# A two-layer hybrid decoder on one core: row and table loads on SyncE's queue, a merged last FFN group, compress in two column halves, and a new issue order

## The chip, the core and the metric

The kernel runs on one core of a Trainium2 chip. The core has five engines that run in parallel, each with its own in-order instruction stream: TensorE (PE, the matmul array; its weight load is listed apart as PEld), VectorE (DVE), ScalarE (ACT), GpSimd (POOL) and SyncE (SP), which here only starts transfers. Sixteen DMA engines move data between HBM and the on-chip memory SBUF; matmuls write to PSUM. The metric is the time of one execution on the device, in microseconds (us); less is better.

## The reference

Two consecutive decoder layers over 256 tokens of 1024 features, in fp32:

```python
for l in range(DEPTH):                                   # 2
    x = LN(a*x + 0.5 * swiglu(x, ffn1_w1, ffn1_w3, ffn1_w2))   # 1024 -> 2816 -> 1024
    z = x @ w_in + b_in                                  # split into 20 parts
    y_a = gmlp(u, v)                                     # causal spatial gating in chunks of 128
    y_b = short_conv(cb, cc, ch)                         # gated convolution, 3 taps
    y_c = mla(q_lat, kv_lat, k_rope)                     # latent attention, 8 heads
    y_d = nsa(nq, nkc, nvc, nks, nvs, nkw, nvw, ngate)   # compressed + selected + window attention
    x = LN(a*x + (sum_i sigmoid(g_i) * y_i) @ w_o)
    x = LN(a*x + cross_attention(x, mem))                # 4 heads, 256 memory rows
    x = LN(a*x + 0.5 * swiglu(x, ffn2_w1, ffn2_w3, ffn2_w2))
```

Inside `nsa`, 15 overlapping blocks of 32 keys and of 32 values are each compressed to one vector for each of two groups: `k_cmp = einsum('bnlgd,lde->bnge', k_blocks + pe_k, wcmp_k)`, and likewise for v. The rows of the result are 2 x 15 = 30, with 64 columns.

## The kernel before

The 256 tokens are two tiles (t = 0, 1) of 128 partitions. All fp32 matmuls of the dense layers are three matmuls of a split form: an operand is a high part (h) and a low part (l), and `mm3` (lines 245 to 250) issues high by high (L248), high by low (L249) and low by high (L250).

**Weights.** `unit` brings a piece of a weight matrix in tiles of 128 x 1024: SP issues the transfer into `raw` (L233, 4 buffers, 0.5 MB), ACT casts it to the high part `wh` (L236), DVE subtracts to the low part `wl` (L237); wh and wl are rings of 8 tiles. `ffn` runs over six column groups of w1 and w3, five of 512 columns and the last of 256; in each group it computes both products for both token tiles, ACT takes silu (L383), DVE multiplies (L385), PE transposes the result (L298), and `wide` multiplies it with w2 into four PSUM tiles (2 token tiles x 2 halves of 512 columns). Weight matrices after that: `z` (the input projections, part by part, each with a bias row), the mixers' projections, `w_o`, cross-attention, the second FFN.

**Small loads.** `row` broadcasts a vector (a bias, the scales gg, gb, qg, and lng and lnb of a layer norm) to 128 partitions; `small` loads a table (ws and bs of the gMLP, cw of the convolution, pek, pev and the compress weights wc). They are issued on POOL, except lng and lnb, which `ln_params` issues on SP. The four pieces of the memory (`memr`, L859) are issued on POOL too. POOL computes besides these only the reciprocal roots of the layer norms (L319) and some gate sums (L814).

**Compress** (lines 556 to 607). For k, and then for v: PE transposes with the 128 x 64 halves of the identity's columns (L569), DVE adds the position table (L579), 16 matmuls with K = 128, 30 stationary columns (kcp) and 64 streamed columns (wc) accumulate into the first 30 partitions of an `att` PSUM tile (L582), and ACT copies it out. k then gets its rotary embedding on DVE, a transpose (L593) and a mask; v is spread to 120 rows by a matmul with a 0/1 matrix `sel` (L600).

**PSUM**: `acc` has 3 buffers, `oacc` 1, `tr` 2, `att` 2, each 128 x 512.

**Order.** Every engine's instruction order is fixed by the table `ISSUE`, which `issue_order` (L965) turns into dependences: for each engine a permutation of its instructions as written. A scheduler chooses nothing here. SP's table gives the order of all transfers on SP's queue; an SP instruction that waits (for a free raw buffer, or a free row buffer) holds those behind it. Around the places that the change moves, in the order of time in layer 0: FFN 1 to about 190 us, its layer norm LN1, the input projections from about 200 us, compress near 280 us, the attention of nsa up to 352 us, the paired transposes of MLA's queries and keys (`mq`, `mk`, in `mla_up`) near 375 us, w_o from 500 us, cross-attention near 570 us, FFN 2 from 587 us. Layer 1 repeats this some 764 us later.

## Time and profile before

| | |
|---|---|
| time, median of 3 runs | 1549.39 us (1548.55 to 1550.39) |
| the profiled execution | 1547.46 us, of which span 1545.6 us |
| granted PE clock, mean | 0.994 of full speed |
| busy: PE / DVE / ACT / POOL | 1501.9 / 1003.0 / 721.0 / 92.2 us |
| SP's DMA queue (q1) | 262.62 MB, 51.3% of the 16 engines' time |
| POOL's DMA queue (q0) | 14.79 MB, 3.8% |

The span is the time from the first to the last instruction on the core, and busy shares are of it. A matmul's duration in a row is longer than the distance to the next one's start, since matmuls overlap in the array; the pace is read from the starts. In a row of the timeline, "x4" means four instructions in one row, and a bracket gives the engine's idle time before it and what ended it.

### The profile page before, as it was taken

The page shows a single profiled execution, that of the slowest core. Times are in us where ns is not written, and L with a number is a line of the kernel's source. Part 1 is how long each engine was busy: PE and PEld are TensorE (multiplying, and loading weights), DVE is VectorE, ACT ScalarE, POOL GpSimd, SP SyncE. Part 2 cuts the span into 40 slices and gives each one's busy share as a digit, 9 for nine tenths or more (in the row PEclk, how much of TensorE's full clock was granted, in tenths as well). Part 3 has the DMA queues.
Part 4 walks back from the last instruction along what each step waited for, and adds up shares of the span by engine and source line. Part 5 has one row for each costly group of instructions (what it writes and reads, how often), then busy time and mean ns, then how long its engine had stood idle before and what let it go on. Part 6 is the DMA issues. An engine that isn't in the chain of part 4 may idle for free.

```text
span 1545.6 us, 20575 instructions
## 1 busy us (share of the span) xinstructions
PE 1501.9 (97%) x7798; PEld 1251.0 (81%) x7798; DVE 1003.0 (65%) x1426; ACT 721.0 (47%) x1060; POOL 92.2 (6%) x116
## 2 busy tenths in 40 slices
PE   7999999998999999999999999999999999999997
PEld 6888878877787888888878888888777888888886
DVE  5556468887865857555566555688878577665644
ACT  5435335554644454444345443355556444544531
POOL 0000011100121000000000000120001300000000
PEclk9999999999999999999999999999999999999999
DMA  8567566434466455556475565764245655356551
GB/s 310 174 205 219 183 210 201 151 100 130 157 206 209 157 184 178 172 173 213 164 231 189 175 214 172 244 192 153 86 145 168 212 191 189 124 191 205 187 188 61
DMA packets 78482, 278.78 MB, mean 180 GB/s; under 512 B 9328, under 2 KB 10032, under 8 KB 78384
## 3 DMA queue, kind: packets, MB, share of 16 engines
q1 hardware_dynamic: 73440, 262.62, 51.3%
q0 software_dynamic: 4800, 14.79, 3.8%
q8 instruction: 61, 1.00, 0.2%
q14 instruction: 37, 0.30, 0.1%
q10 hardware_dynamic: 144, 0.07, 0.0%
HBM read 276.39 MB, written 1.05 MB: 180 GB/s over the span
## 4 chain that ended last, share of the span: by engine, by line
PE 88%; DVE 4%; ACT 3%; DMA 3%; issue 1%; POOLq 0%; ACTq 0%; SPq 0%; DVEq 0%
PE acc L248 23%; PE acc L250 22%; PE acc L249 22%; PE oacc L250 4%; PE oacc L249 4%; PE oacc L248 4%; PE tr L298 3%; DMA raw<-in_wflat_dram 3%; ACT wh L236 2%; PE att L469 1%; DVE wl L237 1%; PE acc L298 1%; PE oacc L482 1%; DVE e L453 1%; PE att L582 0%
## 5 line engine op out<-in xcount | busy, mean ns | idle before, releaser
L237 DVE TENSOR_TENSOR wl<-raw,wh 128x1024 fp32r<-128x1024 f32 (+2 forms) x486 | 581.4, 1208 | 263.4 <-ACT wh L236 254.1
L236 ACT CAST wh<-raw 128x1024 fp32r<-128x1024 f32 (+2 forms) x486 | 501.6, 1041 | 515.8 <-PE acc L250 193.6
L248 PE MATMUL acc<-wh,xh 128*128 128x512 f32 (+3 forms) x1200 | 464.0, 388 | 16.1 <-ACT wh L236 6.9
L249 PE MATMUL acc<-wl,xh 128*128 128x512 f32 (+3 forms) x1200 | 458.6, 383 | 0.0
L250 PE MATMUL acc<-wh,xl 128*128 128x512 f32 (+3 forms) x1200 | 457.0, 382 | 0.1
L248 PEld LDWEIGHTS acc<-wh,xh 128*128 128x128 f32 x1200 | 227.2, 189 | 59.3 <-ACT wh L236 8.6
L250 PEld LDWEIGHTS acc<-wh,xl 128*128 128x128 f32 x1200 | 227.0, 189 | 42.1 <-DVE xl L284 1.6
L249 PEld LDWEIGHTS acc<-wl,xh 128*128 128x128 f32 x1200 | 227.6, 190 | 38.7 <-issue 0.7
L249 PE MATMUL acc<-wl,hh 128*128 128x512 f32 x264 | 103.1, 391 | 0.0
L248 PE MATMUL acc<-wh,hh 128*128 128x512 f32 x264 | 102.8, 389 | 0.0
L250 PE MATMUL acc<-wh,hl 128*128 128x512 f32 x264 | 102.7, 389 | 0.0
L385 DVE SCALAR_TENSOR_TENSOR h<-acc,sil 128x512 f32<-128x512 f32 (+1 forms) x24 | 15.5, 647 | 99.5 <-PE acc L250 99.5
L319 POOL TENSOR_TENSOR rstd<-var,cst 128x1 f32<-128x1 f32 x28 | 28.1, 1004 | 835.1 <-DVE var L318 835.0
L249 PE MATMUL oacc<-wl,xh 128*128 128x512 f32 (+1 forms) x208 | 77.5, 373 | 0.0
L248 PE MATMUL oacc<-wh,xh 128*128 128x512 f32 (+1 forms) x208 | 77.5, 373 | 0.0
L250 PE MATMUL oacc<-wh,xl 128*128 128x512 f32 (+1 forms) x208 | 77.5, 373 | 0.0
L248 PEld LDWEIGHTS acc<-wh,hh 128*128 128x128 f32 x264 | 49.6, 188 | 10.3
L250 PEld LDWEIGHTS acc<-wh,hl 128*128 128x128 f32 x264 | 49.6, 188 | 10.1
L249 PEld LDWEIGHTS acc<-wl,hh 128*128 128x128 f32 x264 | 49.6, 188 | 10.0
L444 ACT ACTIVATE e<-att,nm 128x256 f32<-128x256 f32 (+1 forms) x112 | 46.9, 430 | 9.6 <-DVE nm L440 7.9
L383 ACT ACTIVATE sil<-acc 128x512 f32<-128x512 f32 (+1 forms) x48 | 27.0, 563 | 38.5 <-PE acc L250 38.5
L476 ACT COPY pT<-tr 128x512 f32<-128x512 f32 x36 | 21.1, 586 | 51.1 <-PE tr L298 51.0
(262 smaller groups left out, 1791.7 us busy)
## 6 DMA issues: line engine op xcount, KB each, us to landing
raw<-in_wflat_dram SPq DMA_DIRECT2D x466, 512.0 KB, 5.0
bias<-in_rows_dram POOLq DMA_DIRECT2D x30, 256.0 KB, 4.7
lng<-in_rows_dram SPq DMA_DIRECT2D x8, 512.0 KB, 6.1
lnb<-in_rows_dram SPq DMA_DIRECT2D x8, 512.0 KB, 6.8
raw<-in_wflat_dram SPq DMA_DIRECT2D x8, 416.0 KB, 8.2
wc<-in_small_dram POOLq DMA_DIRECT2D x8, 256.0 KB, 6.0
memr<-in_mem_dram POOLq DMA_DIRECT2D x8, 256.0 KB, 5.4
raw<-in_wflat_dram SPq DMA_DIRECT2D x4, 420.0 KB, 3.9
```

The source lines that it names most:

```text
L236: nc.scalar.copy(hi[:, :m], raw[:, :m])
L237: nc.vector.tensor_sub(lo[:, :m], raw[:, :m], hi[:, :m])
L248: mm(out, ah, bh, start=start, stop=False, skip_group_check=True)
L249: mm(out, ah, bl, start=False, stop=False, skip_group_check=True)
L250: mm(out, al, bh, start=False, stop=stop, skip_group_check=True)
L298: self.nc.tensor.transpose(t[:rows, i * part:(i + 1) * part], s, self.ident[:part, :part])
L319: nc.gpsimd.tensor_tensor(y, v, self.c("mhalf"), op=ALU.pow)
L383: nc.scalar.activation(sil, pa[:, :w], AF.Silu)
L385: nc.vector.scalar_tensor_tensor(h, pb[:, :w], 0.5, sil, op0=ALU.mult, op1=ALU.mult)
L444: nc.scalar.activation(e[:, h * keys:(h + 1) * keys], ps[:, h * keys:(h + 1) * keys], AF.Exp, bias=nm[:, h:h + 1], scale=scale, accum_out= ...
L453: nc.vector.tensor_mul(ev, ev, r[:, :, None].to_broadcast([P, heads, keys]))
L476: nc.scalar.copy(pTs[-1], pt)
```

## The change

Five edits:

- `row`, `small` and the `memr` loads are issued on SP (`nc.sync`) and not on POOL. SP's rows in the order go from 510 to 578, POOL's from 121 to 53.
- The last column group of each FFN takes 256 columns of w1 and 256 of w3 as one unit of 512, into one `acc` tile; silu reads its left half, the product its right half.
- `compress` prepares k and v first, then interleaves their 32 matmuls: k into partitions 0 to 29, v into 64 to 93 of one `att` tile. `sel` moves to partitions 64 to 93.
- `wide` takes (acc, oacc) for t = 0 and (acc, acc) for t = 1 (before: the other way round), and pending transposes are flushed after each of its blocks rather than all before it.
- `ISSUE` is new for all five engines.

```diff
-    def row(self, name, l, o, w, dst, queue=None):
+    def row(self, name, l, o, w, dst):
         base = l * ROW_TOTAL + ROW_OFF[name] + o
-        (queue or self.nc.gpsimd).dma_start(dst, self.a["rows"][0:1, base:base + w].to_broadcast([P, w]))
+        self.nc.sync.dma_start(dst, self.a["rows"][0:1, base:base + w].to_broadcast([P, w]))
...
-        self.nc.gpsimd.dma_start(dst, self.a["small"][:, o:o + w])
+        self.nc.sync.dma_start(dst, self.a["small"][:, o:o + w])
...
-        widths = [512] * 5 + [256]
...
+        for gi in range(6):
+            c0 = gi * 512
+            w = min(512, FF - c0)
+            if w == 512:
+                u1 = self.cols(w1, l, c0, w, KD)
+                u3 = self.cols(w3, l, c0, w, KD)
+            else:
+                u13 = self.cols((w1, w3), l, c0, 2 * w, KD)
             for t in range(NT):
-                pa, pb = self.acc(), self.acc() if t == 0 else self.oacc()
                 self.stream = "af"[t]
-                self.group(pa[:, :w], self.xT[t], u1, 0, w)
-                self.group(pb[:, :w], self.xT[t], u3, 0, w)
+                if w == 512:
+                    pa, pb = self.acc(), self.acc() if t == 0 else self.oacc()
+                    self.group(pa, self.xT[t], u1, 0, w)
+                    self.group(pb, self.xT[t], u3, 0, w)
+                else:
+                    both = self.acc()
+                    self.group(both, self.xT[t], u13, 0, 2 * w)
+                    pa, pb = both[:, :w], both[:, w:]
...
-        self.flush(True)
...
-            po = self.att()
-            for k in range(16):
-                nc.tensor.matmul(po[:30, :64], kcp[:, k * 30:(k + 1) * 30], w[k // 8][:, k % 8 * 64:(k % 8 + 1) * 64],
-                                 start=k == 0, stop=k == 15, skip_group_check=True)
...
+            parts.append((kcp, S[nmw]))
+        po = self.att()
+        for k in range(16):
+            for i, (kcp, w) in enumerate(parts):
+                nc.tensor.matmul(po[64 * i:64 * i + 30, :64], kcp[:, k * 30:(k + 1) * 30],
+                                 w[k // 8][:, k % 8 * 64:(k % 8 + 1) * 64], start=k == 0, stop=k == 15,
+                                 skip_group_check=True)
...
-        out = {t: [self.acc(), self.acc() if t == 0 else self.oacc()] for t in range(NT)}
+        out = {t: [self.acc(), self.oacc() if t == 0 else self.acc()] for t in range(NT)}
...
+                self.flush(True)
...
-                nc.gpsimd.dma_start(mt[t, q], self.a["mem"][t * P:(t + 1) * P, q * 512:(q + 1) * 512])
+                nc.sync.dma_start(mt[t, q], self.a["mem"][t * P:(t + 1) * P, q * 512:(q + 1) * 512])
...
-        "4 0 5-6 1 7 2-3 48-49 8-47 50-78 159-160 79-158 161-172 175-180 173 181 174 182-196 231-232 197-230 "
...
+        "4 0 5-6 1-2 7-47 3 48 50 49 51-58 72 59-61 77 62-71 73-76 78-79 90-92 105 84 87 80 93 81 96-99 101-104 "
```

At the start, SP's order had the constants (cst), lng and lnb right behind the first few weight tiles; now the three stand behind the tiles of the first FFN's w1 and w3. At the end of layer 0's FFN 1, SP issues the first tiles of the input projections (128x1024; those of 128x832 belong to the next part). Its order there was before:

```order
L233 DMA raw_1612<-in_wflat_dram 128x1024
L233 DMA raw_1618<-in_wflat_dram 128x1024
L233 DMA raw_1624<-in_wflat_dram 128x1024
L213 DMA lng_4448<-in_rows_dram 128x1024
L213 DMA lnb_4449<-in_rows_dram 128x1024
L233 DMA raw_1630<-in_wflat_dram 128x1024
L233 DMA raw_1771<-in_wflat_dram 128x832
L233 DMA raw_1777<-in_wflat_dram 128x832
```

and the loads of POOL at that point (two qg, four wc, two bias) were in a queue of their own. Now it is:

```order
L233 DMA raw_1562<-in_wflat_dram 128x1024
L233 DMA raw_1568<-in_wflat_dram 128x1024
L213 DMA gg_1709<-in_rows_dram 128x512
L213 DMA gb_1710<-in_rows_dram 128x512
L218 DMA ws_1711<-in_small_dram 128x512
L213 DMA bias_2073<-in_rows_dram 128x512
L218 DMA pek_1697<-in_small_dram 128x16
L218 DMA pev_1703<-in_small_dram 128x16
L233 DMA raw_1574<-in_wflat_dram 128x1024
L218 DMA bs_1712<-in_small_dram 128x4
L233 DMA raw_1580<-in_wflat_dram 128x1024
```

LN2's lng and lnb are gone from here (they come after the mixers' weights), and gg, gb, ws, one bias, pek, pev and bs have come in, most of them ahead of the tile next to last of the eight (raw_1574; raw_1624 before); qg and wc follow some 20 tiles later.

On PE, compress before had k's 16 products (two rows of 8, by the two wc tiles) ahead of a transpose, with v's behind it (not in this piece):

```order
L250 MATMUL acc_3150<-wh_3110,xl_1569 128x512
L582 MATMUL att_2056<-wc_1749,kcp_2053 30x64 x8
L582 MATMUL att_2056<-wc_1750,kcp_2053 30x64 x8
L697 MATMUL acc_3160<-zv_2203,ws_1761 128x128 x4
L248 MATMUL acc_3150<-wh_3110,xh_1568 128x512
L249 MATMUL acc_3150<-wl_3111,xh_1568 128x512
L250 MATMUL acc_3150<-wh_3110,xl_1569 128x512
L593 MATMUL tr_2083<-ident,cmp_2073 128x30
```

Now k's and v's alternate, here the last of 32, after 32 matmuls of 512 columns since the transposes, and followed by the window attention's scores:

```order
L589 MATMUL att_2021<-wc_1700,kcp_2003 30x64
L589 MATMUL att_2021<-wc_1706,kcp_2018 30x64
L589 MATMUL att_2021<-wc_1700,kcp_2003 30x64
L589 MATMUL att_2021<-wc_1706,kcp_2018 30x64
L250 MATMUL acc_3160<-wh_3156,xl_1488 128x512
L250 MATMUL acc_3196<-wh_3138,xl_1519 128x512
L248 MATMUL acc_3196<-wh_3138,xh_1518 128x512
L474 MATMUL att_2154<-kT_1901,qT_1896 128x128
```

What moved: the products of v came up beside those of k, and the transpose of the compressed keys (L600 now) stands behind eight scores and five matmuls.

On PE, at the end of the nsa attention of layer 0, the products with the values (oacc), the scores with the compressed keys (kcT), the transposes of the exponentials e and the next input projection stood in a row:

```order
L482 MATMUL oacc_2365<-pT_2515,zzd_1927 64x128
L482 MATMUL oacc_2365<-pT_2536,zzd_1927 64x128
L527 MATMUL att_2606<-kcT_2085,qT_1973 128x30 x4
L298 MATMUL tr_2570<-ident,e_2561 128x128 x4
L248 MATMUL acc_3576<-wh_3554,xh_1537 128x512
L249 MATMUL acc_3576<-wl_3555,xh_1537 128x512
L250 MATMUL acc_3576<-wh_3554,xl_1538 128x512
```

Now projection matmuls stand between them:

```order
L487 MATMUL oacc_2313<-pT_2484,zzd_1877 64x128
L248 MATMUL acc_3524<-wh_3502,xh_1487 128x512
L249 MATMUL acc_3524<-wl_3503,xh_1487 128x512
L250 MATMUL acc_3524<-wh_3502,xl_1488 128x512
L248 MATMUL acc_3524<-wh_3502,xh_1487 128x512
L532 MATMUL att_2554<-kcT_2067,qT_1923 128x30 x4
L249 MATMUL acc_3524<-wl_3503,xh_1487 128x512
L250 MATMUL acc_3524<-wh_3502,xl_1488 128x512
...
L250 MATMUL acc_3524<-wh_3508,xl_1488 128x512
L248 MATMUL acc_3524<-wh_3514,xh_1487 128x512
L298 MATMUL tr_2518<-ident,e_2509 128x128 x4
```

Four stand between the products and the scores, and nine between the scores and the transposes; ahead of this piece, two transposes of e, eight scores and eight products follow each other with no projection between. In MLA, the second of the pairs of transposes (tr mq, tr mk) has five projection matmuls between its halves now, and none before; the first pair is as it was. In cross-attention, two output-projection matmuls now stand ahead of the second product with the memory's values (L931 before). The four memr loads stand in SP's order between w_o's fifth and sixth weight tiles.

## Rows read from the trace of the kernel before

**Rows 1.** The page: busy time of each engine; the chain that ended last

```profile
PE 1501.9 (97%) x7798; PEld 1251.0 (81%) x7798; DVE 1003.0 (65%) x1426; ACT 721.0 (47%) x1060; POOL 92.2 (6%) x116
...
PE 88%; DVE 4%; ACT 3%; DMA 3%; issue 1%; POOLq 0%; ACTq 0%; SPq 0%; DVEq 0%
```

**Rows 2.** Timeline of PE in FFN 1: start us, us, instruction, shape, count

```profile
113.52 0.39 PE L249 MATMUL acc<-wl,xh 128*128 128x512 f32 x1
...
114.20 0.39 PE L249 MATMUL acc<-wl,xh 128*128 128x512 f32 x1
...
126.24 0.28 PE L250 MATMUL acc<-wh,xl 128*128 128x256 f32 x1
...
126.96 0.28 PE L250 MATMUL acc<-wh,xl 128*128 128x256 f32 x1
```

**Rows 3.** Timeline of PE: compress, a column-tiled transpose, an untiled product (cross-attention)

```profile
278.86 1.97 PE L582 MATMUL att<-wc,kcp 128*30 128x64 f32 x32
...
282.71 1.09 PE L569 MATMUL tr<-ident,zzb 128*64 128x128 f32 x16
...
569.25 2.05 PE L931 MATMUL acc<-xpT,XV 128*128 128x128 f32 x16 [0.29 <-ACT xpT L927]
```

**Rows 4.** Timelines of SP's queue and of PE at the start

```profile
5.54 0.33 SPq L948 DMA_DIRECT2D cst<-in_consts_dram  x1
...
18.17 0.72 PE L248 MATMUL acc<-wh,xh 128*128 128x512 f32 x2 [1.62 <-ACT wh L236]
```

**Rows 5.** Timelines of POOL's and SP's queues as LN1 ends

```profile
202.94 2.12 POOL L218 DMA_DIRECT2D wc<-in_small_dram  x4
...
203.94 0.33 SPq L213 DMA_DIRECT2D lng<-in_rows_dram  x1
```

**Rows 6.** The chain through that stretch: start us, us, what

```profile
206.49 8.67 DMA raw<-in_wflat_dram
```

**Rows 7.** The page: landing time of weight loads; the cast of a tile

```profile
raw<-in_wflat_dram SPq DMA_DIRECT2D x466, 512.0 KB, 5.0
...
L236 ACT CAST wh<-raw 128x1024 fp32r<-128x1024 f32 (+2 forms) x486 | 501.6, 1041 | 515.8 <-PE acc L250 193.6
```

**Rows 8.** Timeline of PE after LN1 in both layers; in brackets the idle before

```profile
213.21 0.39 PE L248 MATMUL acc<-wh,xh 128*128 128x512 f32 x1
...
216.33 0.80 PE L248 MATMUL acc<-wh,xh 128*128 128x512 f32 x1 [2.74 <-ACT wh L236]
...
219.37 0.39 PE L248 MATMUL acc<-wh,xh 128*128 128x512 f32 x1
...
979.96 0.50 PE L248 MATMUL acc<-wh,xh 128*128 128x512 f32 x1 [2.41 <-ACT wh L236]
```

**Rows 9.** Timeline of PE: end of the sliding-window and compressed attention; an MLA pair

```profile
350.61 0.66 PE L298 MATMUL tr<-ident,e 128*128 128x128 f32 x4 [0.72 <-DVE e L453]
...
352.31 0.79 PE L248 MATMUL acc<-wh,xh 128*128 128x512 f32 x1 [1.04 <-DVE y L739]
...
353.74 0.63 PE L248 MATMUL acc<-wh,xh 128*128 128x512 f32 x1
...
379.17 0.64 PE L298 MATMUL tr<-ident,mk 128*96 128x128 f32 x4 [0.94 <-ACT mk L658]
...
380.86 0.44 PE L248 MATMUL att<-wh,lh 128*128 128x384 f32 x1 [0.28 <-ACT mq L647]
```

**Rows 10.** Timeline of PE in cross-attention and at the start of w_o

```profile
572.60 0.60 PE L931 MATMUL acc<-xpT,XV 128*128 128x128 f32 x3 [0.42 <-ACT xpT L927]
...
501.82 0.50 PE L248 MATMUL acc<-wh,xh 128*128 128x512 f32 x1 [1.54 <-ACT xh L286]
```

**Rows 11.** Table by stretch: us, busy us (instructions) by engine, clock, DMA share, GB/s

```profile
216.33:219.20 2.87, 2.87 (x7) 2.31 (x8) 2.14 (x2) 1.67 (x2) 0.00 (x0) 0.50 0.40 101
...
494.00:500.20 6.20, 6.20 (x32) 5.06 (x30) 5.96 (x9) 3.16 (x3) 0.00 (x0) 1.00 0.58 187
```

**Rows 12.** Waits of SP's queue, 196 to 218 us: total us, times, longest

```profile
SPq L213 <- DVE x L358: 5.8, 1, 5.8
```

More of the change, by code (lines that the diff above doesn't have):

```diff
@@ L98, in _constants @@
     put("cmpvalid", valid)
-    sel = np.zeros((30, 4, 2, NCMP))
+    sel = np.zeros((94, 4, 2, NCMP))
     for g in range(2):
         for n in range(NCMP):
-            sel[g * NCMP + n, :, g, n] = 1.0
+            sel[64 + g * NCMP + n, :, g, n] = 1.0
     put("sel", sel)
@@ L335, in ln_params @@
         b = self.p.tile([P, D], F32, name=self.nm("lnb"), tag="lnb", bufs=1)
-        self.row(f"ln{which}_g", l, 0, D, g, nc.sync)
-        self.row(f"ln{which}_b", l, 0, D, b, nc.sync)
+        self.row(f"ln{which}_g", l, 0, D, g)
+        self.row(f"ln{which}_b", l, 0, D, b)
         return g, b
@@ L557, in compress @@
         nc = self.nc
-        outs = []
+        parts = []
         for i, (nmw, nmp) in enumerate((("wck", "pek"), ("wcv", "pev"))):
-            w, pe = S[nmw], S[nmp]
+            pe = S[nmp]
             kc = self.s("kc2")
@@ L579, in compress @@
                 nc.vector.tensor_add(kpv[:, :, g, :], src, pe[:, :, None].to_broadcast([P, 16, NCMP]))
-            po = self.att()
-            for k in range(16):
-                nc.tensor.matmul(po[:30, :64], kcp[:, k * 30:(k + 1) * 30], w[k // 8][:, k % 8 * 64:(k % 8 + 1) * 64],
-                                 start=k == 0, stop=k == 15, skip_group_check=True)
-            c = self.s("cmp", P)[:30]
-            if i == 0:
-                kr = self.s("kraw", 64)[:30]
-                nc.scalar.copy(kr, po[:30, :64])
-                cv = c.rearrange("p (u d) -> p u d", u=2)
-                x = kr[:, None, :]
-                self.rope(cv[:, 0:1, :], x, self.c("rcc", 30), self.c("rcs", 30), 1, 32, rows=30)
-                nc.vector.tensor_copy(cv[:, 1, :], cv[:, 0, :])
-                pt = self.tr()
-                nc.tensor.transpose(pt[:, :30], c, self.ident[:30, :30])
-                kcT = self.s("kcT", 30)
-                nc.vector.tensor_mul(kcT, pt[:, :30], self.c("bd"))
-                outs.append(kcT)
-            else:
-                nc.scalar.copy(c[:, :64], po[:30, :64])
-                pr = self.tr()
-                nc.tensor.matmul(pr[:120, :64], self.c("sel", 30), c[:, :64], start=True, stop=True,
-                                 skip_group_check=True)
-                vr = self.s("vrep")[:120]
-                nc.vector.tensor_mul(vr.rearrange("p (h d) -> p h d", h=8),
-                                     pr[:120, None, :64].to_broadcast([120, 8, 64]),
-                                     self.c("blk", 120)[:, :, None].to_broadcast([120, 8, 64]))
-                outs.append(vr)
@@ L607, in compress @@
-        return outs
+            parts.append((kcp, S[nmw]))
[4 more added lines that the diff above has]
+                                 w[k // 8][:, k % 8 * 64:(k % 8 + 1) * 64], start=k == 0, stop=k == 15,
+                                 skip_group_check=True)
+        c = self.s("cmp", P)
+        kr = self.s("kraw", 64)[:30]
+        nc.scalar.copy(kr, po[:30, :64])
@@ new lines, in compress @@
+        nc.scalar.copy(c[64:94, :64], po[64:94, :64])
+        cv = c[:30].rearrange("p (u d) -> p u d", u=2)
+        self.rope(cv[:, 0:1, :], kr[:, None, :], self.c("rcc", 30), self.c("rcs", 30), 1, 32, rows=30)
+        nc.vector.tensor_copy(cv[:, 1, :], cv[:, 0, :])
+        pt = self.tr()
+        nc.tensor.transpose(pt[:, :30], c[:30], self.ident[:30, :30])
+        kcT = self.s("kcT", 30)
+        nc.vector.tensor_mul(kcT, pt[:, :30], self.c("bd"))
+        pr = self.tr()
+        nc.tensor.matmul(pr[:120, :64], self.c("sel", 94)[64:], c[64:94, :64], start=True, stop=True,
+                         skip_group_check=True)
@@ L609, in mla_latents @@
+        vr = self.s("vrep")[:120]
+        nc.vector.tensor_mul(vr.rearrange("p (h d) -> p h d", h=8),
+                             pr[:120, None, :64].to_broadcast([120, 8, 64]),
+                             self.c("blk", 120)[:, :, None].to_broadcast([120, 8, 64]))
+        return kcT, vr
     def mla_latents(self, S):
@@ L1110, in _layout, with cut @@
     W["nsa_wout"] = W["nsa_wout"][:, WOUT_ROWS, :]
+    def cut(n, l, k0, nk, c0, w):
+        if isinstance(n, tuple):
+            return np.concatenate([cut(m, l, k0, nk, c0, w // len(n)) for m in n], 1)
+        return W[n][l, k0 * P:(k0 + nk) * P, c0:c0 + w]
     flat = np.concatenate([
-        W[n][l, k0 * P:(k0 + nk) * P, c0:c0 + w].reshape(nk, P, w).transpose(1, 0, 2).reshape(-1)
-        for n, l, k0, nk, c0, w in plan])
+        cut(n, l, k0, nk, c0, w).reshape(nk, P, w).transpose(1, 0, 2).reshape(-1) for n, l, k0, nk, c0, w in plan])
     rows, small = [], []
```

10 lines of the change are left out of this document (2 added, 8 removed), and 227 rows, old and new, of the table ISSUE.

## The prediction

> **What bounds the kernel now.** I read the busy row and the chain first: TensorE (PE) works 97% of the span, and the chain that ended last is 88% PE [rows 1]. So an edit pays only if it shortens PE's own work or one of its waits; DVE, ACT and the DMA rings matter where PE waits for them. The idle time in front of PE is about 44 us (span less busy), and the timelines of PE show where it stands: a few places of 0.4 to 2.7 us that come back in both layers. The terms below are those places and the two edits to PE's work.
>
> **FFN tail, 256 to 512 columns.** Four FFNs, two token tiles, w1 and w3, eight k, three matmuls each: 384 matmuls of 256 columns go, 192 of 512 columns come. In one stretch the 256-column ones start 0.72 us apart over six, 0.120 each; the 512-column ones 0.68 apart over three, 0.227 each [rows 2]. 384 x 0.120 = 46.1 and 192 x 0.227 = 43.6: **2.5 us saved**, all on PE's path. Weight bytes stay the same. The silu and the product now wait for one group instead of two; their cover is the first blocks of w2, which need earlier h tiles, so I cost that at nothing; uncovered it would be a wait like the 0.72 to 1.04 us of [rows 9] per FFN.
>
> **Compress in two halves.** Before, k and v each run 16 matmuls, which the trace counts as 32 (two fp32 passes), in 1.97 us; two layers, so four such stretches [rows 3]. After, k writes partitions 0 to 29 and v 64 to 93, alternating. What speaks for an overlap is line 569, which alternates column halves already: 16 in 1.09 us, while the untiled line 931, with the same 128 streamed columns, takes 2.05 us for 16 [rows 3]. If the compress halves overlap as well, 4 x 1.97 becomes 2 x 1.97, less a little for the first pair: **3.6 us saved**. Bounds: at best 3.9; at worst each matmul costs what one of line 569 costs, 1.09 / 16 = 68 ns, and 128 of them take 8.7 us instead of 7.9, a loss of 0.8. I take 3.6, since 569 streams twice as many columns. The Trainium skill, "TensorEngine Tiling (Array Packing)", Instruction Overhead, speaks against it: every matmul carries some 60 cycles, and a tiling factor should not be taken from a dimension that is already small, as 64 columns and 30 weights are; by that rule the term is about zero. No run here shows so short a stream in halves. The merged compress also waits until both inputs are ready; the order has 32 matmuls of 512 columns between its transposes and its products and 13 matmuls between the products and the next transpose, so I add nothing (uncovered: one wait for e or y as below, about 1 us per layer).
>
> **The start.** The constants and, behind them, LN1's lng and lnb, 0.5 MB each, are issued ahead of a weight tile, and PE then waits 1.62 us for that tile's cast [rows 4]. In the new order all three stand behind the first FFN's w1|w3 tiles, so the tile lands 1.5 MB earlier: **1.6 us saved**. What is late next is the tile after it, which moves up alike.
>
> **After LN1, where the projections begin.** This is the largest place. Around 203 us POOL issues qg, four wc and two bias loads, and SP issues lng and lnb of LN2 [rows 5]; the weight tile issued behind them at 206.49 needs 8.67 us to land [rows 6], where the median is 5.0 [rows 7]. PE idles 2.74 us for its cast, and after that idle time it runs at a granted clock of 0.50 (1.2 instead of 2.4 GHz) [rows 11]: the seven matmuls from 216.33 to 219.37 take 3.04 us instead of 7 x 0.227 = 1.59 [rows 8]. Together 2.74 + 1.45 = 4.2. Layer 1 has the same with 2.41 idle [rows 8]: 3.9, if the low clock costs as much there. In the new SP order lng and lnb stand after the mixers' weights, qg and wc some 20 tiles later; gg, gb, ws and one bias (1 MB) stand ahead of the tile before it, but what they wait for is done earlier on PE than the release of that one, so they go out while the rings have time. With 5.0 to land from 206.49 and 1.04 for the cast [rows 7] the tile is ready at 212.5; PE needs it at 213.4. **8.0 us saved**, with 0.9 us to spare; if half of the delay stays, half of the gain is lost. The zc bias now comes later and could hold DVE's evacuation; PE has some 4 us of other groups there, so nothing is added.
>
> **End of the sliding-window and compressed attention.** Before, scores, transposes of e and the next projection stand back to back: PE idles 0.72 us for e and 1.04 us for y, and three matmuls at the low clock cost 1.43 instead of 0.68 [rows 9]. The new order puts four matmuls behind the attention products and nine or more 512-column ones between the compressed scores and the transposes of e (2 us of cover against 1.8 of idle): 0.72 + 1.04 + 0.75 = 2.5, twice: **5.0 us saved** (layer 1 taken as layer 0). But the stretch ahead of it (two transposes of e, eight scores, eight products) now has no filler: there I add two waits like the 0.72 in each layer, **2.9 us lost**; bounds 0 and 6.
>
> **MLA pairs.** tr mq and tr mk stood back to back, with 0.94 us of idle for mk and 0.28 for mq in each of two pairs [rows 9]. The first pair stays as it was; in the second five matmuls (1.1 us) stand between: 1.2, twice: **2.4 us saved**. **Cross-attention:** two output-projection matmuls now stand ahead of the second product, which waits 0.42 us [rows 10]; twice: **0.8 us saved**.
>
> **w_o.** Here the move can cost. The four memr loads (1.05 MB) went out on POOL's queue before the w_o tiles; now they stand in SP's queue among them, and PE already waits 1.54 us there [rows 10]. In the 6.2 us before that wait the rings are 0.58 busy at 187 GB/s [rows 11]: 0.42 x 6.2 us at 322 GB/s (187 / 0.58) is room for 0.84 MB; 0.21 MB is left over, 0.65 us. Bounds: nothing, or all of it, 1.05 MB at 322 GB/s = 3.3 us. I take 1.0 per layer: **2.0 us lost**.
>
> The out-tile swap in wide() and the flush in its blocks change which PSUM buffer comes free first; PE's order shows the same matmuls around the layer norms, so zero, with 1 us either way.
>
> **Sum:** 2.5 + 3.6 + 1.6 + 8.0 + 5.0 + 2.4 + 0.8 - 2.9 - 2.0 = 19.0 us. The profiled execution took 1547.46 and would take 1528.5; the median of the runs is 1.9 above it, so 1530.
>
> **Rivals.** *A, the halves do not overlap* (the change does not do what it says): +3.6, 1533.7. *B, the burst only moves.* A load is as heavy on SP's queue as on POOL's; if the 1 MB that now stands ahead of the tile is still in flight at 206, PE waits as before: +8.0, 1538. The Trainium skill, "DMA: Bandwidth & Descriptors", Issuing engines are not separate DMA queues, says that all issuers share the same 16 engines, so that only the order and not the queue can help; the row of 8.67 us agrees, and by that rule alone the change of queue gains nothing. *C, the rearranged stalls come back* (next to another product): 5.0 + 2.4 + 0.8 = 8.2, 1538. *D, slower: a row load blocks the weights.* SP issues in order; 68 more loads stand in its queue, and a load that waits for its buffer holds every weight tile behind it. The queue's own waits show it: a row load (L213) held it 5.8 us for a DVE result of the layer norm [rows 12], and the tile behind came late. Each such hold that empties the ring costs about 4.2 (idle and clock); five undo the gain, six give 1530 + 25 = 1555. Against it: in the built program nearly every row load waits for something that PE has passed before it reaches what the next weight tile waits for; the exception is lnb ahead of the last FFN, 35 matmuls later.
>
> **How the numbers follow.** 0.2% (3 us) is about what a measurement of this kernel can tell from no change. Forecast 0.50 (own range 1524 to 1536: no new waits and no loss at w_o, 4.9 less; both at their upper bounds, 3.1 and 4.6 more, one of them, and 1 of the swap); A 0.14; B 0.10; C 0.12, all faster; two or three of A to C at once, up to 1530 + 20 = 1550, 0.05 (same); D 0.09 (slower). Faster 0.86, same 0.05, slower 0.09. The range reaches from 1520 (other waits that I counted nothing for go too) to 1544 (two of the rivals at once).
>
> **What would show it.** In the profile after: 192 fewer matmuls and no 256-column form with x; compress in about 2 us per layer with starts some 28 ns apart (A: 56); no idle before PE near 18; after LN1 a tile that lands in 5 us, no PE row with an idle over 1 us there and a full granted clock (B: the same 2 to 3 us); no row of 0.72 and 1.04 before the compressed transposes, 0.5 to 0.7 before the products ahead; w_o's idle at 2 to 3 us instead of 1.54. D would show as waits of SP's queue at L213 followed by PE idle for wh. The prediction is wrong if idle of PE after stays above 35 us, or if it falls under 15.

## The result and the profile after

The changed kernel takes 1529.1 us (median of 4 runs, 1527.79 to 1532.97) against 1549.89 before: ratio 0.9871, interval 0.9851 to 0.9891. The forecast was 1530. The profiled execution took 1528.15, of which the span is 1526.4; the sum in the prediction gave 1528.5.

The page after, as in [rows 1]: busy time (share) and count of each engine, and the chain that ended last; then the group of the 512-column matmuls with the idle time in front of them and what ended most of it.

```profile
PE 1489.9 (98%) x7606; PEld 1234.3 (81%) x7606; DVE 1002.8 (66%) x1426; ACT 719.9 (47%) x1060; POOL 50.6 (3%) x48
...
PE 88%; DMA 4%; DVE 3%; ACT 3%; issue 1%; SPq 0%; POOLq 0%; POOL 0%; ACTq 0%; DVEq 0%
L248 PE MATMUL acc<-wh,xh 128*128 128x512 f32 (+2 forms) x1168 | 461.3, 396 | 8.5 <-ACT xh L286 4.2
```

192 matmuls fewer, as said. PE is busy 12.0 us less and idle 7.2 us less (span less busy: 43.7 before, 36.5 after). Half of the idle in front of the 512-column products is now for `xh`, the cast of the transposed gated sum at the start of w_o.

Where the time went by stage. A stage ends where PE starts the first matmul on the newly normalised x, a row that both timelines have (before 199.56, 540.24, 587.04, 774.81, 963.51, 1302.65, 1349.53; after 197.40, 530.38, 576.75, 764.01, 953.47, 1285.00, 1331.88); the last stage ends with the span. The column "forecast" puts the prediction's terms into their stages.

| stage | before, us | after, us | change | forecast |
|---|---|---|---|---|
| start and FFN 1, layer 0 | 199.56 | 197.40 | -2.2 | -2.2 |
| projections, mixers, w_o, layer 0 | 340.68 | 332.98 | -7.7 | -7.2 |
| cross-attention, layer 0 | 46.80 | 46.37 | -0.4 | -0.4 |
| FFN 2, layer 0 | 187.77 | 187.26 | -0.5 | -0.6 |
| FFN 1, layer 1 | 188.70 | 189.46 | +0.8 | -0.6 |
| projections, mixers, w_o, layer 1 | 339.14 | 331.53 | -7.6 | -7.0 |
| cross-attention, layer 1 | 46.88 | 46.88 | 0.0 | -0.4 |
| FFN 2, layer 1, to the end | 196.07 | 194.52 | -1.6 | -0.6 |
| sum | 1545.6 | 1526.4 | -19.2 | -19.0 |

The stages agree with the forecast to within 1.4 us each; inside the two long ones some terms are wrong, and cancel. Of the 1.6 us of the last stage, 1.0 lies behind PE's last matmul (9.8 us from its start to the end of the span before, 8.8 after, and about the same in every run of the changed kernel below); its cause is open. The rows, in the order of the prediction. First the timeline of PE after at compress and at the start (start us, us, instruction, shape, count, idle before it in brackets), the places of [rows 3] and [rows 4].

```profile
281.00 1.98 PE L589 MATMUL att<-wc,kcp 128*30 128x64 f32 x64
...
15.45 0.73 PE L248 MATMUL acc<-wh,xh 128*128 128x512 f32 x2 [0.28 <-ACT wh L236]
```

64 matmul records (the 32 products of k and v) in the time that 32 took: two column halves with 30 stationary columns and 64 streamed ones overlap fully. At the start 0.28 us of idle is left of 1.62.

The stretch behind LN1 in both layers, in the table by stretch (us, then busy us with instructions for PE, PEld, DVE, ACT, POOL, then granted clock, DMA share, GB/s), to be read against [rows 8] and [rows 11].

```profile
197.40:216.00 18.60, 18.58 (x84) 15.07 (x85) 16.45 (x23) 7.01 (x9) 0.99 (x1) 1.00 0.53 169
953.47:972.00 18.53, 18.51 (x84) 15.02 (x85) 15.88 (x22) 6.96 (x9) 0.92 (x1) 1.00 0.53 167
```

PE is busy throughout, at the full granted clock (2.4 GHz): the idles of 2.74 and 2.41 us and the seven slow matmuls behind are gone in both layers.

The end of the sliding-window attention in the timeline of PE, layer 0 (337 to 343 us) and layer 1, and the clock of the stretch behind the first two; the counterpart of [rows 9].

```profile
337.20 0.63 PE L298 MATMUL tr<-ident,e 128*128 128x128 f32 x4 [1.79 <-DVE e L458]
338.81 1.12 PE L298 MATMUL acc<-ident,zcb 128*128 128x128 f32 x4 [0.98 <-DVE y L742]
343.19 1.09 PE L487 MATMUL oacc<-pT,zzd 128*64 128x128 f32 x14 [0.31 <-ACT pT L481]
...
1093.67 1.16 PE L474 MATMUL att<-kT,qT 64*128 64x128 f32 x14 [1.74 <-ACT e L449]
...
338.80:341.90 3.10, 3.09 (x21) 2.54 (x21) 2.02 (x4) 1.14 (x5) 0.00 (x0) 0.51 0.34 52
```

The waits of 0.72 and 1.04 us ahead of and behind the compressed transposes are gone. In layer 0 the waits ahead of them, 1.79 and 0.98, are larger than those removed; in layer 1 one wait of 1.74, for ACT's e, stands for the two.

MLA in the timeline of PE, layer 0 and then layer 1; DVE's row behind the wait for T; the chain's row ahead of that (start us, us, what); and SP's queue ahead of this load.

```profile
365.75 0.61 PE L298 MATMUL tr<-ident,mq 128*96 128x128 f32 x4 [0.69 <-DVE mq L432]
367.31 0.64 PE L298 MATMUL tr<-ident,mk 128*96 128x128 f32 x4 [0.94 <-ACT mk L661]
371.62 0.50 PE L248 MATMUL acc<-wh,yah 128*128 128x512 f32 x1 [0.80 <-DVE T L802]
...
1119.89 0.64 PE L298 MATMUL tr<-ident,mk 128*96 128x128 f32 x4 [0.94 <-ACT mk L661]
1124.34 0.64 PE L298 MATMUL tr<-ident,mk 128*96 128x128 f32 x4 [0.94 <-ACT mk L661]
...
370.87 0.69 DVE L802 TENSOR_TENSOR T<-acc,bias 128x512 f32<-128x512 f32 x1 [0.94 <-DMA bias<-in_rows_dram]
...
364.62 6.23 DMA bias<-in_rows_dram
...
349.85 14.71 SPq L233 DMA_DIRECT2D raw<-in_wflat_dram  x6
```

In MLA's attention, PE before waited four times for DVE's e, twice in each layer (timeline of PE before); the changed kernel has no such wait of 0.2 us or more there.

```profile
410.94 0.63 PE L298 MATMUL tr<-ident,e 128*128 128x128 f32 x4 [0.51 <-DVE e L453]
415.95 0.63 PE L298 MATMUL tr<-ident,e 128*128 128x128 f32 x4 [0.50 <-DVE e L453]
...
1174.80 0.63 PE L298 MATMUL tr<-ident,e 128*128 128x128 f32 x4 [0.52 <-DVE e L453]
1179.57 0.63 PE L298 MATMUL tr<-ident,e 128*128 128x128 f32 x4 [0.24 <-DVE e L453]
```

The start of w_o in both layers (layer 1 before, then both after), and two waits in layer 1's FFN 1 that were not there before (timeline of PE), with DVE's rows at the first of them.

```profile
1264.64 0.50 PE L248 MATMUL acc<-wh,xh 128*128 128x512 f32 x1 [0.95 <-ACT xh L286]
...
492.11 0.50 PE L248 MATMUL acc<-wh,xh 128*128 128x512 f32 x1 [1.92 <-ACT xh L286]
1245.92 0.50 PE L248 MATMUL acc<-wh,xh 128*128 128x512 f32 x1 [2.32 <-ACT xh L286]
...
781.70 0.66 PE L298 MATMUL acc<-ident,h 128*128 128x128 f32 x4 [0.69 <-DVE h L391]
791.56 0.66 PE L298 MATMUL tr<-ident,h 128*128 128x128 f32 x4 [0.77 <-DVE h L391]
...
779.82 1.23 DVE L237 TENSOR_TENSOR wl<-raw,wh 128x1024 fp32r<-128x1024 f32 x1 [2.69 <-ACT wh L236]
780.96 0.68 DVE L391 SCALAR_TENSOR_TENSOR h<-acc,sil 128x512 f32<-128x512 f32 x1
```

### The profile page after: what moved, and what is told of

Its sections match the earlier page's. It is cut to its first block, busy times and chain, and to the rows that moved or that the text cites. A ratio compares the mean times of both kernels' runs of the same rounds, so it can differ in the third digit from the quotient of the medians.

```text
span 1526.4 us, 20113 instructions
## 1 busy us (share of the span) xinstructions
PE 1489.9 (98%) x7606; PEld 1234.3 (81%) x7606; DVE 1002.8 (66%) x1426; ACT 719.9 (47%) x1060; POOL 50.6 (3%) x48
## 4 chain that ended last, share of the span: by engine, by line
PE 88%; DMA 4%; DVE 3%; ACT 3%; issue 1%; SPq 0%; POOLq 0%; POOL 0%; ACTq 0%; DVEq 0%
PE acc L248 22%; PE acc L250 22%; PE acc L249 22%; PE oacc L248 4%; PE oacc L249 4%; PE oacc L250 4%; PE tr L298 3%; DMA raw<-in_wflat_dram 3%; DVE wl L237 2%; ACT wh L236 2%; PE att L474 2%; PE oacc L487 1%; PE acc L298 1%; PE acc L935 1%; PE att L919 0%
## 5 line engine op out<-in xcount | busy, mean ns | idle before, releaser
L248 PE MATMUL acc<-wh,xh 128*128 128x512 f32 (+2 forms) x1168 | 461.3, 396 | 8.5 <-ACT xh L286 4.2
L250 PE MATMUL acc<-wh,xl 128*128 128x512 f32 (+2 forms) x1168 | 454.9, 390 | 0.1
L249 PE MATMUL acc<-wl,xh 128*128 128x512 f32 (+2 forms) x1168 | 454.5, 390 | 0.0
L248 PEld LDWEIGHTS acc<-wh,xh 128*128 128x128 f32 x1168 | 220.0, 188 | 52.3 <-ACT xh L283 6.0
L250 PEld LDWEIGHTS acc<-wh,xl 128*128 128x128 f32 x1168 | 219.8, 188 | 44.3 <-DVE xl L284 1.6
L249 PEld LDWEIGHTS acc<-wl,xh 128*128 128x128 f32 x1168 | 220.2, 189 | 39.9 <-issue 0.2
L249 PE MATMUL oacc<-wl,xh 128*128 128x512 f32 x176 | 68.7, 390 | 0.0
L248 PE MATMUL oacc<-wh,xh 128*128 128x512 f32 x176 | 68.7, 390 | 0.0
L250 PE MATMUL oacc<-wh,xl 128*128 128x512 f32 x176 | 68.5, 389 | 0.0
L319 POOL TENSOR_TENSOR rstd<-var,cst 128x1 f32<-128x1 f32 x28 | 23.6, 846 | 1112.2 <-DVE var L318 1111.9
```

The source lines that it names most:

```text
L248: mm(out, ah, bh, start=start, stop=False, skip_group_check=True)
L249: mm(out, ah, bl, start=False, stop=False, skip_group_check=True)
L250: mm(out, al, bh, start=False, stop=stop, skip_group_check=True)
L319: nc.gpsimd.tensor_tensor(y, v, self.c("mhalf"), op=ALU.pow)
```

## The experiments

The time of one kernel moves from run to run by more than most terms are large: the two profiled executions of the changed kernel below are 4.5 us apart. So small terms are read from the row at their place, and medians where a whole kernel is compared. Where an edit of the issue order goes with a piece of code, the pieces below show the main lines alone ("..." marks what is left out).

**The changed kernel again,** beside three of the kernels below.

> The changed kernel once more, beside the three below. If the medians on record stand, 1529 us (1527 to 1533) and 19 to 20 us under the kernel before. The stalls that moved with the change should be at the same places: PE idle 1.8 and 1.0 us near 337 and 339 for e and y, 1.7 us near 1094 for e, 1.9 and 2.3 us at the start of w_o (492 and 1246). What may differ from run to run is the granted clock in the few microseconds behind such an idle: up to 3 us in all.

Measured: 1529.75 us (1525.93 to 1532.76, 5 runs), ratio 0.9884 (0.9865 to 0.9903); the kernel before, measured beside it, 1547.33. The stalls that were named are at the same places within 0.25 us (1.78 and 0.98; 1.74; 2.14 and 2.13 at w_o); the first wait for h in layer 1 is 1.14 instead of 0.69. The profiled execution is 4.5 us longer than the first one. Set against the first matmul by matmul, 2.7 us of it lie where the granted clock differs: 1.5 behind w_o's wait in layer 0 and 1.2 behind the wait of 1.74 us in layer 1. Another 1.2 lie at the start, where the matmuls stand 0.43 us apart until 10.6 us in the first profile and until 13.0 us in this one. An example of the clock is the stretch behind the wait of 1.74 us (PE goes on at 1093.67 and at 1097.44) in the table by stretch, first the earlier profile, then this one.

```profile
1093.60:1097.00 3.40, 3.02 (x32) 2.49 (x34) 3.30 (x10) 1.75 (x6) 0.00 (x0) 1.00 0.02 5
...
1097.00:1101.00 4.00, 3.56 (x24) 2.83 (x24) 3.90 (x10) 1.47 (x4) 0.00 (x0) 0.69 0.01 4
```

**Layer norm rows later, in the kernel before.** Only SP's order is edited, LN2's lng and lnb in both layers; qg, wc and the biases stay on POOL. `moved` puts positions a to b-1 ahead of position c.

```diff
+MOVES = {'SP': [(79, 81, 155), (330, 332, 399)]}
+def moved(order, moves):
+    at = list(range(len(order)))
+    for a, b, c in moves:
+        part = [i for i in at if a <= i < b]
+        at = [i for i in at if not a <= i < b]
+        j = at.index(c)
+        at[j:j] = part
+    return [order[i] for i in at]
...
+        order = moved(order, MOVES.get(engine, ()))
```

> The kernel before, with one edit to SP's order: LN2's lng and lnb of both layers are issued some 70 tiles later, among the mixers' weights, as in the changed kernel. POOL still issues qg, wc and the biases on its own queue at 202 us. Theory (what counts is how many bytes stand ahead of the weight tile): 1.0 MB less at about 0.41 MB/us, so the tile issued near 206 us lands 2.5 us earlier, near 212.7 instead of 215.2; PE's idle there falls from 2.74 and 2.41 us to 0.5 or less in each layer and the low clock behind it goes, so 6 to 8 us less than before: 1541.5 to 1543.5. Rival (the queue counts: POOL's loads slow SP's tiles because two queues share the rings): the idle stays above 1.5 us in each layer and the time falls by less than 3 us.

Measured: 1543.44 us (1541.33 to 1548.2, 10 runs) against 1548.0, ratio 0.9967 (0.9948 to 0.9987). The timeline of PE behind LN1 in layer 0 and layer 1, and at LN2 in layer 0:

```profile
215.48 0.50 PE L248 MATMUL acc<-wh,xh 128*128 128x512 f32 x1 [0.77 <-ACT wh L236]
...
974.55 0.50 PE L248 MATMUL acc<-wh,xh 128*128 128x512 f32 x1 [0.53 <-ACT wh L236]
...
536.87 0.50 PE L248 MATMUL acc<-wh,xh 128*128 128x512 f32 x1 [1.68 <-ACT xh L283]
```

2.74 became 0.77 and 2.41 became 0.53, and the slow matmuls behind are gone: about 6 us of the 8 come from 1 MB per layer that no longer stands ahead of a weight tile, with the queues as they were. LN2's own wait grew (1.23 to 1.68 us in layer 0, 0.82 to 1.74 in layer 1), which takes back 1.4; the median gains 4.6. So the order of bytes pays, without a change of queue. In the changed kernel, where qg and wc stand later too, the rest of the 8 us went as well; which of these loads it was, no run tried alone.

**k's 16 products, then v's,** in the changed kernel, in the same two column halves.

```diff
-        for k in range(16):
-            for i, (kcp, w) in enumerate(parts):
+        for i, (kcp, w) in enumerate(parts):
+            for k in range(16):
```

> The changed kernel, with one edit: in compress k's 16 products are issued first and v's 16 behind them, into the same two halves of the array and the same tile. Theory (neighbours in different halves overlap): starts 56 ns apart instead of 28, so 128 matmuls take 7.2 us instead of 3.8, and the kernel is 3.4 to 3.7 us slower than the changed one. Rival (the gain came from joining the two batches and from the halves as such): starts stay at 28 ns and the time does not change.

Measured: 1535.73 us (1534.94 to 1536.33), ratio 0.9923 (0.9899 to 0.9947). In the timeline of PE:

```profile
282.69 3.56 PE L589 MATMUL att<-wc,kcp 128*30 128x64 f32 x64
```

3.56 against 1.98 us, 56 ns instead of 28 between starts: alternation alone makes the overlap, worth 1.6 us per layer by these rows. The median moved by 6.6, twice what the two layers make. In the profile the rest lies at other places, in waits (0.70 us for h at 27.7, 1.01 for a transposed projection at 998.7, 1.49 ahead of cross-attention in layer 1) and in the clock behind them. All four runs were slower than every run of the changed kernel; whether the edit brings these waits is not shown.

**The merged last group, each matmul as two of 256 columns,** in the changed kernel. The sums of the last group's gate and product come out with other values here; the columns multiplied are those of the changed kernel, in pieces.

```diff
-                self.mm3(out, ah, al, bh, bl, i == 0, i == kt - 1)
+                for j, (p, q) in enumerate(((ah, bh), (ah, bl), (al, bh))):
+                    for n in (0, 256):
+                        self.nc.tensor.matmul(out[:, n:n + 256], p, q[:, n:n + 256], start=i + j == 0,
+                                              stop=i == kt - 1 and j == 2, skip_group_check=True)
...
-                    self.group(both, self.xT[t], u13, 0, 2 * w)
+                    self.group(both, self.xT[t], u13, 0, 2 * w, halves=True)
...
```

> The changed kernel, with one edit: in the merged last group of the FFNs each matmul of 512 columns is issued as two of 256 columns with the same stationary operand, 384 instead of 192. Theory: 0.120 us for each instead of 0.227 for two, so 46.1 instead of 43.6 us: 2.5 us slower than the changed kernel. Rival (the merged group gains by the single evacuation or by its place in the order, not by the matmuls): less than 1 us.

Measured: 1537.22 us (1531.88 to 1538.43), ratio 0.9926 (0.9897 to 0.9956). Set against the changed kernel's trace matmul by matmul, it falls back by 0.57 us at each of the four FFN tails: 2.3 us, against 2.5 forecast for the whole term. The other 8 us of the profiled span lie at places that the edit does not touch (the start, 530, 992 to 1104, 1244 us), in waits and the clock behind them; whether the edit brings them is not shown.

**The memory's pieces (memr) on POOL again,** behind the gate sums, in the changed kernel.

```diff
-                nc.sync.dma_start(mt[t, q], self.a["mem"][t * P:(t + 1) * P, q * 512:(q + 1) * 512])
+                nc.gpsimd.dma_start(mt[t, q], self.a["mem"][t * P:(t + 1) * P, q * 512:(q + 1) * 512])
...
```

> The changed kernel, with the four memr loads of each layer back on POOL's queue, behind the gate sums as before; all else as changed. Theory (1.05 MB among w_o's weight tiles delays the cast in front of w_o): PE's idle at w_o's start falls from 1.92 and 2.32 us to about 1.5 and 1.0, and the low clock in layer 1 goes: 2 to 3 us faster than the changed kernel. Rival (w_o waits for something else that the new order brought): idle and time unchanged.

Measured: 1528.86 us (1527.11 to 1535.37), ratio 0.9875 (0.9846 to 0.9903); against 1529.75 of the changed kernel no difference that can be read, so the 2 to 3 us did not come. In the timeline of PE the idle at w_o is 1.81 in layer 0 (1.92 with memr on SP), and in layer 1 it halves:

```profile
1254.59 0.50 PE L248 MATMUL acc<-wh,xh 128*128 128x512 f32 x1 [1.20 <-ACT xh L286]
```

So memr alone explains most of what was added in layer 1 (2.32 to 1.20, with 0.95 before the change), and little in layer 0.

**The convolution's taps cut short,** in the changed kernel: line 738 on 2 of 128 columns, which leaves out most of the gated short convolution (`short_conv` of the reference; the expectation calls it the compress convolution).

```diff
-                    nc.vector.scalar_tensor_tensor(yv[:, f, :], zt[:, f, k:k + P], cwv[:, f, k:k + 1], yv[:, f, :],
+                    nc.vector.scalar_tensor_tensor(yv[:, f, :2], zt[:, f, k:k + 2], cwv[:, f, k:k + 1], yv[:, f, :2],
```

> The changed kernel, but the second and third taps of the compress convolution (line 738) work on 2 of 128 columns, so most of the convolution is left out and each of those DVE instructions takes some 0.07 us instead of 0.35. Theory (the waits at the end of sliding-window attention did not go, they moved: DVE, busy with the taps, is late with the row maxima, e and y): the idles near 337.2 (1.79), 338.8 (0.98) and 1093.7 (1.74) fall under 0.7 each, 2 to 2.6 us less in all, 1526.5. Rival (the wait is the chain scores, maximum, exponent, scaling itself, whatever else DVE does): the same idles within 0.3 us, 1529.

Measured: 1527.16 us (1525.29 to 1529.97), ratio 0.9872 (0.9849 to 0.9894). The median lies near the theory's 1526.5, but the gain is not at the places that it named (0.6 us of it is a wait of 0.69 for mq at 365.7 that became 0.11). Each of the shortened instructions took 0.22 us, not the 0.07 expected (0.35 whole), so DVE was relieved by less than half of what was meant. By the rows the theory fell all the same: timeline of PE,

```profile
337.83 0.63 PE L298 MATMUL tr<-ident,e 128*128 128x128 f32 x4 [1.78 <-DVE e L458]
339.17 1.12 PE L298 MATMUL acc<-ident,zcb 128*128 128x128 f32 x4 [0.71 <-DVE y L742]
```

and 1.74 again in layer 1. Less work on DVE shortens only the wait for y, by 0.27. What PE waits for is the chain itself, in DVE's timeline of the changed kernel:

```profile
335.30 0.17 DVE L452 RECIPROCAL r<-sm 128x2 f32<-128x2 f32 x1 [0.20 <-ACT e L449]
335.50 0.16 DVE L455 TENSOR_TENSOR rg<-r,gate 128x2 f32<-128x2 f32 x1
335.57 0.69 DVE L443 TENSOR_REDUCE mx<-att 128x2 f32<-128x512 f32 x1
336.30 0.17 DVE L445 TENSOR_SCALAR nm<-mx 128x2 f32<-128x2 f32 x1
336.37 0.68 DVE L458 TENSOR_TENSOR e<-e,rg 128x512 f32<-128x512 f32 x1
```

DVE waits for ACT's exponential (0.20 us idle), so the taps ahead of it do not hold the chain here; then it takes the next pair's maximum before it scales e. The same five stand in this order in the kernel before; there eight scores with the compressed keys (1.08 us on PE) stood between the products and these transposes, and the wait was 0.72. They have moved away: 0.72 + 1.08 = 1.80, and the row says 1.79. From nm to the end of the scaled e the chain takes 3.1 us in both kernels. No run put the scores back, or e ahead of the next pair's maximum. In layer 1 the wait of 1.74 is for ACT's e, and this account does not cover it.

**ACT's order,** in the changed kernel: xh ahead of the last cast (w_o, FFN 2) or of KT (cross-attention), both layers; and the same **with memr on POOL**.

```diff
+MOVES = {'Activation': [(324, 326, 323), (791, 793, 790), (344, 346, 343), (811, 813, 810), (381, 383, 380), (848, 850, 847)]}
```

> The changed kernel with six swaps in ACT's order alone: the copies xh of the transposed x go ahead of the last weight cast (w_o, last FFN) or of the copy KT (cross-attention) that stands in front of them, in both layers. Theory (at these boundaries PE waits for xh because ACT is in a cast that PE needs later): the idle at w_o falls from 1.9 and 2.3 to about 0.9 and 1.1, at the cross-attention projections from 1.1 and 0.3 to 0.6 and 0, at the last FFN from 0.6 to about 0.1 in both layers; 4 to 5 us less with the clock behind w_o, 1524.5. Rival (the cast that now stands behind is the next thing PE waits for): the same idle comes 2 to 4 matmuls later, under 1.5 us less, 1528.

> As the run with ACT's six swaps, and the memr loads on POOL behind the gate sums. Theory (at w_o two things were late one behind the other, the tile's cast and xh behind it; with xh ahead, the memory tiles no longer matter): within 0.5 us of the run with the swaps alone, 1524.5. Rival (the memr loads among the w_o tiles delay the weights, and these are late once xh is not): another 1 to 2 us less, all of it within 10 us behind the start of w_o, 1523.

Measured: 1526.7 us (1525.81 to 1529.64) with the swaps, ratio 0.9868 (0.985 to 0.9887); 1524.38 us (1523.32 to 1528.69) with memr on POOL as well, ratio 0.9855 (0.9835 to 0.9876); the changed kernel beside them 1529.75. Of the 4 to 5 us forecast for the swaps 3.0 came. w_o in the timelines of PE, the two layers of the first and of the second:

```profile
491.84 0.50 PE L248 MATMUL acc<-wh,xh 128*128 128x512 f32 x1 [0.74 <-ACT xh L286]
1247.04 0.50 PE L248 MATMUL acc<-wh,xh 128*128 128x512 f32 x1 [1.24 <-ACT xh L286]
...
493.32 0.50 PE L248 MATMUL acc<-wh,xh 128*128 128x512 f32 x1 [0.25 <-ACT xh L286]
1247.70 0.50 PE L248 MATMUL acc<-wh,xh 128*128 128x512 f32 x1 [0.25 <-ACT xh L286]
```

My theory for the second was wrong and its rival right, by these rows (the two ranges of times overlap): memr among the w_o tiles delays the casts, and the cast delays xh. Either alone leaves 0.7 to 1.8 us, both together 0.25. In the changed kernel the row on ACT shows the link:

```profile
490.51 1.04 ACT L236 CAST wh<-raw 128x1024 fp32r<-128x1024 f32 x1 [0.37 <-DMA raw<-in_wflat_dram]
491.47 1.08 ACT L286 ACTIVATE xh<-tr 128x512 fp32r<-128x512 f32 x2
```

At FFN 2's start no idle of 0.25 us or more is left (0.6 in both layers); at cross-attention nothing is gained, since a wait for xl follows (0.74 and 0.64 us in the run with the swaps).

**The start's order taken back,** in the changed kernel: cst, lng and lnb ahead of the third unit's tile.

```diff
+MOVES = {'SP': [(47, 49, 7), (50, 51, 7)]}
```

> The changed kernel, with the constants and LN1's lng and lnb issued again where they were, ahead of the weight tile of the third unit. Theory (the 1.62 us of idle at the start was 1.5 MB that stood ahead of a tile): an idle of about 1.6 us comes back before the first or second use of that tile's cast, between 15 and 19 us, in place of 0.28; 1.3 us more, 1530.5, of which only the local row can be read with certainty. Rival (the start is bound by the rings as a whole, whatever stands first): the same idle as in the changed kernel, at most 0.3 us more, 1529.

Measured: 1531.16 us (1530.19 to 1531.64), ratio 0.9886 (0.9866 to 0.9905). In the timeline of PE:

```profile
18.18 0.74 PE L248 MATMUL acc<-wh,xh 128*128 128x512 f32 x2 [1.50 <-ACT wh L236]
```

1.50 us against 0.28: the term is the order of these three loads. The median is 1.4 and 2.1 us over the two of the changed kernel (1529.75 and 1529.1).

**Five swaps more,** on top of ACT's six and memr on POOL: xl and h ahead of one wl each on DVE, one cast behind pT and two e on ACT.

```diff
-MOVES = {'Activation': [(324, 326, 323), (791, 793, 790), (344, 346, 343), (811, 813, 810), (381, 383, 380), (848, 850, 847)]}
+MOVES = {'Activation': [(324, 326, 323), (791, 793, 790), (344, 346, 343), (811, 813, 810), (381, 383, 380), (848, 850, 847), (677, 680, 676)], 'DVE': [(727, 728, 726), (734, 735, 733), (552, 554, 551), (1264, 1266, 1263)]}
```

> The changed kernel with memr on POOL and ACT's six swaps, and five more swaps: in DVE's order the low half xl of the transposed x ahead of one wl in the cross-attention projections of both layers, the product h ahead of one wl at two places of the third FFN's tail; in ACT's order a weight cast behind one pT and two e in the second layer. Theory (each of these waits of PE is an instruction held by a wl or a cast that PE needs later): idles at 532 and 1287 (1.0 and 0.7) fall under 0.3, at 782 and 792 (0.6 and 0.8) under 0.1, at 1094 from 1.7 to about 1.2; 3 us under the run without the five swaps, 1521.5. Rival (the wl that is now later is what PE needs next): the idles return within ten matmuls, 1524.4 again.

Measured: **1521.71 us** (1520.85 to 1522.23), ratio 0.9824 (0.9808 to 0.9841) to the kernel before, 7.4 us under the 1529.1 of the changed kernel: the best of all, and as forecast (1521.5). The two waits in FFN 1 of layer 1 and the wait for xl at 1287 are gone, 1.74 became 1.24. One came back elsewhere, in the timelines of PE and of ACT:

```profile
538.88 0.66 PE L298 MATMUL tr<-ident,xq 128*128 128x128 f32 x4 [1.91 <-ACT xq L912]
...
537.30 1.04 ACT L236 CAST wh<-raw 128x1024 fp32r<-128x1024 f32 x1 [2.36 <-DMA raw<-in_wflat_dram]
538.25 0.58 ACT L912 COPY xq<-acc 128x512 f32<-128x512 f32 x1
```

A cast that waits for its tile holds xq behind it. Whether the swap of xl in layer 0 makes that tile late, or it is late in some runs anyway (0.50 at the same place with ACT's swaps alone, none with memr on POOL as well), was not tried.

## Why the prediction was right, and where its steps were not

- **FFN tail, -2.5:** right; cutting the matmuls again costs 2.3.
- **Compress, -3.6:** right; 1.96 us per layer are gone (3.9 in all, the upper bound), and the alternation is worth 1.6 of it per layer when it alone is undone; the other 0.4 comes with the joined batches (3.56 us against 2 x 1.97). Rival A fell: at 64 streamed and 30 stationary columns the rows show starts 28 ns apart, half of 56. The Trainium skill, "TensorEngine Tiling (Array Packing)", Instruction Overhead, warns that every matmul carries a fixed cost and that a tiling factor should not be taken from a small dimension; at this shape the rows do not bear the warning out. (Rival A's time is 1530 + 3.6 = 1533.6, not 1533.7; nothing hangs on it.)
- **The start, -1.6:** right in place; 1.34 measured, since 0.28 of the idle stayed.
- **After LN1, -8.0:** right; no idle and no slow matmul is left in either layer. Rival B fell: the order of the bytes alone brought about 6 of the 8 (experiment with the layer norm rows), with POOL's loads still in their own queue. The Trainium skill, "DMA: Bandwidth & Descriptors", Issuing engines are not separate DMA queues, says that DMAs run on the same 16 DMA engines whichever engine issues them. That experiment agrees, though no run here changed the queue of these loads and left their place in time.
- **End of the attention, -5.0 and +2.9:** the kinds were right and the sizes not. The waits at the compressed transposes went. I priced the two new waits per layer at 0.72, a wait that still had 1.08 us of scores as cover; without the cover it is 1.79 in layer 0, and y another 0.98 behind it, with the clock low after (0.51). There the waits for e and y that I counted as removed came back ahead of another product, as rival C has it; in layer 1 a single wait of 1.74 did. Idle and what the low clock costs together: layer 0 went from about 3.5 to 4.7 us, layer 1 from about 4.1 to 2.1. The net is about -1, not -2.1.
- **MLA, -2.4:** this step failed; the net is +0.2. I read the new order in layer 0 and took layer 1 as alike, but there both pairs stand back to back still, with the old 0.94 each. In layer 0 the waits did leave the second pair; 0.69 for mq ahead of the first and 0.80 for T in the second took their place (2.42 us of waits before, 2.69 after). The latter is a wait that I had ruled out for another bias: a bias load, now in SP's queue, is issued at 364.62, behind six weight loads that were held up for free buffers from 349.85 on, and lands 6.23 us later. In the runs of the changed kernel and its variants this wait is 0.4 to 2.4 us, and absent in one; no run moved that load. It is the mirror of rival D: not a row load that blocks the weights, but a weight load that blocks a row.
- **Not in the sum:** the four waits of DVE for e in MLA's attention, 0.51, 0.50, 0.52 and 0.24 us before (near 411, 416, 1175 and 1180), are gone: 1.8 us, with the granted clock at 1.00 behind them. Nothing in the prediction named them, and why they went was not tried. They cover for most of MLA's -2.4 in the stages' sum, which is luck.
- **Cross-attention, -0.8:** right; both waits of 0.42 for xpT are gone. In layer 1, 0.72 for xl (0.26 before) took it back.
- **w_o, +2.0:** right in sign, small in size. Idle +0.4 in layer 0 (1.54 to 1.92) and +1.4 in layer 1 (0.95 to 2.32), with some 1.5 lost at the low clock behind the latter: +3.3. What I named, memr, was half of the cause; ACT's order was the other.
- **FFN 1 of layer 1, nothing in the sum, +1.5:** h stands on DVE behind a wl that waits 2.69 us for the cast of its tile. In the last experiment h went ahead of that wl, and both waits were gone.
- **The mark of 35 us of idle was set badly.** My own terms lower the idle to 43.7 less the idle parts (1.6 + 5.2 + 3.5 + 2.4 + 0.8) plus 4.9 of new waits: 35.1, so the mark stood on the forecast itself, and 36.5 is over it while the time is right. The low clock's part of the gain shows as busy time.

Counted by these rows, the terms come to -13.6 of -19.2: -2.3, -3.9, -1.3, -8.0, -1.0, +0.2, -1.8, -0.3, +3.3, +1.5. Three more that the timelines show add -2.1: LN2's waits (1.23 and 0.82 us before, 1.09 and 0.29 after), a wait of 0.36 for mk near 393 that is gone, and the 1.0 at the end of the span. The remaining 3.5 us is spread over places too short to single out, and stays open. So the large terms were right for the reasons given, but that the total came within 1 us of the forecast is in part luck: errors of both signs, and gains that no term named, made up for MLA, w_o and FFN 1.

## What to carry to other kernels

Ask of each load in an in-order queue what stands ahead of it and how long that may be held: here a move to SP's queue mattered by the tiles that it put a load behind (the bias) or ahead of (memr). When a filler is moved away from a wait, the wait can grow by the filler's whole length (0.72 to 1.79 us here), so price it without the cover, and read the new order in every layer: a hand-written order need not repeat. When a wait has two causes in a row, a late load and an instruction queued behind it, removing one shows little; try both.

## What the runs showed of the hardware that I had not expected

Two column halves of the array overlap fully even with 30 stationary and 64 streamed columns: 64 matmul records in 1.98 us, 28 ns from start to start. And after the same idle of 1.74 us the granted clock falls in one execution and not in the next, 1.00 and 0.69 in the two profiles of the same kernel above; at two such places together the clock makes 2.7 us of the 4.5 between them.
